# Delta rule: block turns on VectorE and hops through a DRAM buffer in place of TensorE transposes and repeats

## The chip, the cores and the metric

The kernel runs on one core of a Trainium2 chip. The metric is the device time of one execution in microseconds; a kernel's time is the median of its runs. Beside the runs there is one profiled execution, and its rows are what the profile shows. TensorE multiplies matrices, VectorE and ScalarE work elementwise, GpSimd does small copies and issues some DMAs, and SyncE (SP) issues most DMAs. Each engine takes its instructions in order.

## The reference

One inference step of one decoder layer, for 256 prompt tokens and 32 sample tokens (8 sequences of 4), in float32:

```python
proj = x @ w_in                       # 2048 -> 11280 columns: gB gC h q k v z b a m_a m_b
y_a = (gB * conv3(gC * h)) @ w_a_out
q, k, v = split(silu(conv4(concat(q, k, v))))
q, k = l2norm(q), l2norm(k)           # per head, 8 heads of 128
beta = sigmoid(b);  g = -exp(a_log) * softplus(a + dt_bias)
o, S = gated_delta_rule(q, k, v, g, beta, S0)
o = o * rsqrt(mean(o * o) + eps) * gdn_norm_w * silu(z)
y_b = o @ w_b_out
x = layer_norm(ALPHA * x + (sig(m_a) * y_a + sig(m_b) * y_b) @ w_o)
x = layer_norm(ALPHA * x + relu(x @ w_up)**2 @ w_down)
```

The delta rule works on chunks of 64 tokens. Per head and chunk it builds a 64x64 triangular matrix from the keys, inverts it, and then walks the chunks with a state S of 128x128:

```python
v_new = u - w @ S
o     = qdec @ S + attn @ v_new
S     = S * exp(glast) + kdec.T @ v_new
```

The prompt has four chunks and starts from S = 0; each sample sequence is one short chunk and starts from its own S0. The outputs are the prompt's and samples' rows, the convolutions' last inputs and the new states.

## The kernel before

**Weight blocks.** All projections are one list of 496 blocks. A block is 512 KB of weights, loaded by SP (line 171) into one of four buffers. ScalarE rounds it to a high half (`hi`, line 179), VectorE subtracts that to get a low half (`lo`, line 186), and TensorE multiplies each 128x128 piece three times (lines 206 to 208): high by high, high by low, low by high. The activations lie turned, with features in the 128 partitions and 288 tokens along the free axis. In the main loop (line 1371), the iteration of block i makes the high half of block i+3, runs one step of the delta rule, makes the low half of block i+3, runs the evacuations that fall due, multiplies block i and issues the load of block i+7. The order on every engine is thus written out by hand.

**Order of the blocks.** First k, q, v of heads 0 to 3 (blocks 0 to 23), then of heads 4 to 7 (24 to 47), then the inputs of mixer A (48 to 95), z (96 to 111), and the merge. Four blocks make a group of 256 columns. Its evacuation (`conv_evac`, line 253) runs in the three blocks after it: GpSimd writes the padding (lines 265, 266), ScalarE copies from PSUM, VectorE does three multiply-adds per 128 columns (line 272), ScalarE applies SiLU. The z group's evacuation (`z_evac`, line 354) multiplies the delta rule's outputs in the tile `ao` in place, two heads at a time, for heads 0 and 1 at block 100, then at 104, 108 and 112.

**The delta rule.** `gdn(G)` (line 919) is a generator that runs twice, for heads 0 to 3 and 4 to 7; each `yield` ends a step, and the main loop takes one step per block. The first half begins in block 20. The second begins when the first is done and its samples' program too. Its parts, with lines of the kernel before:

- Lines 924 to 926: the samples' states S0 (2 MB per half) are loaded by four DMAs that GpSimd issues, at step 0.
- Lines 954 to 965: keys and queries lie as features x tokens. TensorE turns them by 16 transposes per half (line 958); ScalarE squares them and copies the keys to `kdec` (lines 960, 962); VectorE sums the squares (line 963).
- Lines 973 to 987: the samples' keys and queries are turned (two transposes); the samples' keys, repeated four times by GpSimd (`wide`, line 976), are turned by four more (line 980).
- Lines 995 to 1042: decays, norms, the products of keys with keys and queries.
- Lines 1045 to 1121: the triangular inverse. Its first step needs `mx`, of which GpSimd makes the low part (line 1089) after `spread_kq` (line 1063); TensorE takes it at line 1094. `states_of` (line 1068) multiplies S0 by the samples' keys and queries.
- Lines 1136 to 1207: `sample()`, a second generator that runs one step per block beside the first. It solves the samples' small system, repeats the values four times by four matmuls (line 1176), makes `vm` on GpSimd (line 1192) and adds eight products to S0 (line 1203), two per step, each in a PSUM tile of its own.
- Lines 1215 to 1221: values are turned by eight transposes per half.
- Lines 1226 to 1267: the walk over the chunks. `p3` (two tiles) and `p4` (one) hold products in PSUM and are released by VectorE (lines 1262 and 1264).
- Lines 1272 to 1299: the outputs are normalised and turned back by eight transposes per half into `ao`; the samples' part by one.

There are four PSUM tiles of this kind (`gtile`, line 124), taken in turn. A small pool of tags is shared: a new tile of a tag waits until the old one's readers are done.

Of the kernel before, what the change touches and what calls it, by code (L numbers as in the profile page):

```python
# [16 lines left out]
P = 128  # L17
# [86 lines left out]
def hybrid_kernel(ctx: ExitStack, tc: tile.TileContext, A):  # L104
# [11 lines left out]
    gp = pool("gp", 4, space=PSUM)  # L116

# [798 lines left out]
    def four(ap):  # L916
        return ap.rearrange("p (h t) -> p h t", h=4).unsqueeze(2).to_broadcast([P, 4, 4, 32])

    def gdn(G):
# [4 lines left out]
        S0 = pl.tile([P, 4, 8, P], F32, tag="S0", name=nm("S0"))  # L924
        for hh in range(4):
            gps.dma_start(S0[:, hh], A["state_gdn"][0, :, 4 * G + hh].rearrange("b d e -> d b e"))

# [11 lines left out]
        rep4 = sqr[:, 512:1024]  # L939
        junk = sqr[:, 192:320]  # L940
        wide = rep4.rearrange("p (h q t) -> p h q t", h=4, q=4)
# [7 lines left out]
        red = T([P, 4, 4], "red")  # L949
# [4 lines left out]
        for c in range(4):  # L954
            kt = gtile()
            kv = kt.rearrange("p (h c) -> p h c", h=4)
            for hh in range(4):
                pe.transpose(kv[:, hh, :], kq[:, hh, c].rearrange("p s x -> p (s x)"), ident)  # L958
            s2 = sqr[:, 512 * (c % 2):512 * (c % 2) + 512].rearrange("p (h c) -> p h c", h=4)
            act.activation(s2, kv, AF.Square)  # L960
            for par in range(2):
                act.copy(kdec[rows[par], c], kv[rows[par], par::2, :])
            dve.tensor_reduce(out=red[:, c, :], in_=s2, axis=mybir.AxisListType.X, op=ADD)
# [4 lines left out]
        ssv = ss[:, 0:16].rearrange("p (a c r) -> p a c r", a=2, c=4)  # L968
        for par in range(2):
            act.copy(ssv[rows[par], 0], red[rows[par], :, par::2])  # L970
            act.copy(ssv[rows[par], 1], red[rows[par], :, 1 - par::2])
        sp2 = gtile()
        pe.transpose(sp2[:, 0:128], kst, ident)
        pe.transpose(sp2[:, 128:256], qst, ident)

        gps.tensor_copy(wide, four(kst))
        yield
        ktr = gtile()
        for hh in range(4):
            pe.transpose(ktr[:, hh * P:hh * P + P], rep4[:, hh * P:hh * P + P], ident)  # L980
        kr = T([P, 4, P], "kr")
        for u in range(2):
            act.activation(junk, sp2[:, u * P:u * P + P], AF.Square, accum_out=ss[:, 16 + u:17 + u])
# [471 lines left out]
```

## Time and profile before

| what | value |
|---|---|
| runs, median (lowest to highest) | 1708.3 us (1707.88 to 1708.3), 3 runs |
| profiled execution, from first to last instruction | 1703.4 us |
| mean granted TensorE clock | 0.998 |
| instructions | 31106 |
| bytes moved by DMA | 279.18 MB, mean 164 GB/s |
| delta rule, first transposes of the first half | at 92.8 us |
| delta rule, last transpose of the second half | at 436.3 us |

The profiled execution's own time outside the span is not recorded; the median of the runs stands 4.9 us above the span. A row of a group of instructions gives line, engine, operation, the tiles written and read, their shape and count, then the busy time, the mean of one in ns, and the idle time before them with what ended it. A row of the timeline gives start and length in us, and in brackets the idle time before it. A row of the chain in order of time gives start and length of one piece of the chain that ended last. A row of a window gives, for a stretch of time, the busy us of TensorE, its weight loads, VectorE, ScalarE and GpSimd with their instruction counts, then granted clock, DMA share and GB/s. A row of a DMA gives tiles, issuing queue, count, size and the median us from issue to landing.

### The profile page before, as it was taken

The page shows a single profiled execution, that of the slowest core. Times are in us where ns is not written, and L with a number is a line of the kernel's source. Part 1 is how long each engine was busy: PE and PEld are TensorE (multiplying, and loading weights), DVE is VectorE, ACT ScalarE, POOL GpSimd, SP SyncE. Part 2 cuts the span into 40 slices and gives each one's busy share as a digit, 9 for nine tenths or more (in the row PEclk, how much of TensorE's full clock was granted, in tenths as well). Part 3 has the DMA queues.
Part 4 walks back from the last instruction along what each step waited for, and adds up shares of the span by engine and source line. Part 5 has one row for each costly group of instructions (what it writes and reads, how often), then busy time and mean ns, then how long its engine had stood idle before and what let it go on. Part 6 is the DMA issues. An engine that isn't in the chain of part 4 may idle for free.

```text
span 1703.4 us, 31106 instructions
## 1 busy us (share of the span) xinstructions
PE 1688.5 (99%) x13063; PEld 1668.7 (98%) x13063; DVE 1007.2 (59%) x1296; ACT 734.1 (43%) x1067; POOL 133.8 (8%) x223
## 2 busy tenths in 40 slices
PE   9999999999999999999999999999999999999997
PEld 7999999999999999999999999999999999999997
DVE  5577876758544444456778844566445654466565
ACT  4675626333543333334445533444334433344442
POOL 2232412023300000000010000000000000000000
PEclk9999999999999999999999999999999999999999
DMA  8464456435555555555565555555555555555552
GB/s 244 140 194 139 123 175 200 150 115 180 162 170 169 166 162 170 163 164 165 158 190 174 165 170 161 164 170 162 167 168 161 163 171 162 164 167 164 162 162 80
DMA packets 275097, 279.18 MB, mean 164 GB/s; under 512 B 13131, under 2 KB 270092, under 8 KB 274952
## 3 DMA queue, kind: packets, MB, share of 16 engines
q1 hardware_dynamic: 270414, 265.95, 51.3%
q0 software_dynamic: 4256, 11.12, 2.3%
q8 instruction: 102, 1.67, 0.4%
q14 instruction: 37, 0.30, 0.1%
q10 hardware_dynamic: 288, 0.13, 0.0%
HBM read 269.68 MB, written 7.48 MB: 163 GB/s over the span
## 4 chain that ended last, share of the span: by engine, by line
PE 98%; DVE 1%; DMA 0%; POOL 0%; issue 0%; SPq 0%; ACT 0%; POOLq 0%; ACTq 0%
PE acc L206 31%; PE acc L208 31%; PE acc L207 31%; PE g L1084 1%; DMA xr<-in_x_prompt_dram 0%; PE g L1072 0%; PE g L1231 0%; PE g L1251 0%; PE g L831 0%; DVE w L143 0%; PE g L1254 0%; PE g L1203 0%; PE g L1243 0%; PE g L608 0%; PE g L798 0%; PE g L958 0%
## 5 line engine op out<-in xcount | busy, mean ns | idle before, releaser
L140 DVE TENSOR_TENSOR lo<-raw,hi 128x1024 fp32r<-128x1024 f32 (+2 forms) x502 | 614.0, 1226 | 556.2 <-ACT hi L179 553.7
L179 ACT CAST hi<-raw 128x1024 fp32r<-128x1024 f32 (+1 forms) x498 | 517.6, 1041 | 765.0 <-PE acc L207 707.7
L206 PE MATMUL acc<-xh,hi 128*128 128x288 f32 x1408 | 422.9, 300 | 0.0
L208 PE MATMUL acc<-xh,lo 128*128 128x288 f32 x1408 | 416.7, 296 | 0.0
L207 PE MATMUL acc<-xl,hi 128*128 128x288 f32 x1408 | 416.5, 296 | 0.0
L206 PE MATMUL acc<-dh,hi 128*128 128x290 f32 x1024 | 303.9, 297 | 0.0
L207 PE MATMUL acc<-dl,hi 128*128 128x290 f32 x1024 | 303.3, 296 | 0.0
L208 PE MATMUL acc<-dh,lo 128*128 128x290 f32 x1024 | 302.7, 296 | 0.0
L206 PE MATMUL acc<-hh,hi 128*128 128x288 f32 x1024 | 302.3, 295 | 0.0
L208 PE MATMUL acc<-hh,lo 128*128 128x288 f32 x1024 | 302.3, 295 | 0.0
L207 PE MATMUL acc<-hl,hi 128*128 128x288 f32 x1024 | 302.3, 295 | 0.0
L206 PEld LDWEIGHTS acc<-xh,hi 128*128 128x128 f32 x1408 | 265.4, 189 | 2.6 <-issue 0.7
L207 PEld LDWEIGHTS acc<-xl,hi 128*128 128x128 f32 x1408 | 265.8, 189 | 0.5
L208 PEld LDWEIGHTS acc<-xh,lo 128*128 128x128 f32 x1408 | 265.6, 189 | 0.0
L206 PEld LDWEIGHTS acc<-dh,hi 128*128 128x128 f32 x1024 | 193.6, 189 | 0.1
L208 PEld LDWEIGHTS acc<-dh,lo 128*128 128x128 f32 x1024 | 193.3, 189 | 0.0
L207 PEld LDWEIGHTS acc<-dl,hi 128*128 128x128 f32 x1024 | 193.3, 189 | 0.1
L207 PEld LDWEIGHTS acc<-hl,hi 128*128 128x128 f32 x1024 | 192.5, 188 | 0.0
L208 PEld LDWEIGHTS acc<-hh,lo 128*128 128x128 f32 x1024 | 192.3, 188 | 0.0
L206 PEld LDWEIGHTS acc<-hh,hi 128*128 128x128 f32 x1024 | 192.1, 188 | 0.0
L207 PE MATMUL acc<-ml,hi 128*128 128x288 f32 x256 | 75.6, 295 | 0.0
L208 PE MATMUL acc<-mh,lo 128*128 128x288 f32 x256 | 75.6, 295 | 0.0
(404 smaller groups left out, 1620.0 us busy)
## 6 DMA issues: line engine op xcount, KB each, us to landing
raw<-in_w_in_dram SPq DMA_DIRECT2D x176, 512.0 KB, 3.5
raw<-in_w_up_dram SPq DMA_DIRECT2D x128, 512.0 KB, 3.9
raw<-in_w_down_dram SPq DMA_DIRECT2D x128, 512.0 KB, 3.7
raw<-in_w_o_dram SPq DMA_DIRECT2D x32, 512.0 KB, 3.7
raw<-in_w_a_out_dram SPq DMA_DIRECT2D x16, 512.0 KB, 3.7
raw<-in_w_b_out_dram SPq DMA_DIRECT2D x16, 512.0 KB, 3.6
S<-in_state_gdn_dram POOLq DMA_DIRECT2D x8, 512.0 KB, 7.8
out_dram<-S POOLq DMA_DIRECT2D x8, 512.0 KB, 4.9
```

The costliest lines, as they stand in the source:

```text
L140: dve.tensor_tensor(out=out, in0=a, in1=b, op=op)
L179: act.copy(his[i][:, k:k + step], raw[i][:, k:k + step])
L206: pe.matmul(o, wh, xh_, start=st, stop=False)
L207: pe.matmul(o, wh, xl_, start=False, stop=False)
L208: pe.matmul(o, wl, xh_, start=False, stop=en)
L1084: pe.matmul(out[r, q * 64:q * 64 + 64], a[r, q, :], b[r, q, :], start=True, stop=True)
```

## The change

A DRAM buffer `dp` is added. VectorE's transpose turns each 32x32 block of a tile in its place, so a full 128x128 turn also needs the blocks to change places; DMAs do that on the way to DRAM and back.

- Keys and queries: VectorE turns blocks into `tk` (steps 0 and 1), four SP DMAs write them to `dk` (step 2), four SP DMAs read them back as `kT` and `qT` (step 3). ScalarE squares each in one instruction of 1024 columns, VectorE sums it (step 5). `kdec` is made from `kT` by the multiply that was there.
- Samples' keys and queries: one block turn, eight GpSimd DMAs to `ds` (step 1), one read into `spk` and four reads into `kr` (step 3), which repeat the keys.
- Values: two block turns (step 10), four SP writes (step 11), one SP read (step 12) into `v`, which now lies as four pieces of 32 columns.
- Samples' values: ScalarE copies them out of PSUM, one GpSimd write to `dx`, four GpSimd reads that repeat them.
- Outputs: two block turns into `to`, four SP writes to `do`, eight SP reads into `ao` in pieces of 32 tokens (128 bytes).
- `tk`, `qT`, `kT` and `tv` share the memory of S0 (tag `S0`). S0 is therefore loaded later, at step 13 of the half, when they have been read.
- Step counts: a half has 48 steps after the first instead of 47 (first) and 41 instead of 40 (second); `sample()` begins at step 24 instead of 22 and has three steps more.

The diff, cut to its core:

```diff
+    dp = pool("dp", space=bass.MemoryType.DRAM)
...
-        S0 = pl.tile([P, 4, 8, P], F32, tag="S0", name=nm("S0"))
-        for hh in range(4):
-            gps.dma_start(S0[:, hh], A["state_gdn"][0, :, 4 * G + hh].rearrange("b d e -> d b e"))
...
-        for c in range(4):
-            kt = gtile()
-            kv = kt.rearrange("p (h c) -> p h c", h=4)
-            for hh in range(4):
-                pe.transpose(kv[:, hh, :], kq[:, hh, c].rearrange("p s x -> p (s x)"), ident)
-            s2 = sqr[:, 512 * (c % 2):512 * (c % 2) + 512].rearrange("p (h c) -> p h c", h=4)
-            act.activation(s2, kv, AF.Square)
-            for par in range(2):
-                act.copy(kdec[rows[par], c], kv[rows[par], par::2, :])
-            dve.tensor_reduce(out=red[:, c, :], in_=s2, axis=mybir.AxisListType.X, op=ADD)
-            if c % 2:
+        for hh in range(4):
+            dve.transpose(out=tk[:, :, hh % 2, :, hh // 2],
+                          in_=kq[:, hh].rearrange("p c s x -> p c (s x)").rearrange("p c (j b) -> p j c b", j=4))
+            if hh == 1:
+                dve.transpose(out=ts.rearrange("p u h x -> p (u h x)"), in_=kqs.rearrange("p u h b t -> p (u h b t)"))
+            if hh == 1:
                 yield
+        ds = dp.tile([P, 2, P], F32, tag="ds", name=nm("ds"))
+        for u in range(2):
+            for i in range(4):
+                gps.dma_start(ds[:, u, rows32(i)].rearrange("(h b) x -> b h x", h=4), ts[rows32(i), u])
+        yield
+        dk = dp.tile([P, 4, 2, 256], F32, tag="dk", name=nm("dk"))
+        for i in range(4):
+            sp.dma_start(dk[:, i].rearrange("(j b) a t -> b j (a t)", j=4),
+                         tk[rows32(i)].rearrange("p j a c r x -> p j (a c r x)"))
+        gps.dma_start(spk, ds)
+        for q in range(4):
+            gps.dma_start(kr[rows32(q)], ds[:, 0].rearrange("(h b) d -> b h d", h=4))
...
+        for a in range(2):
+            r = rows[a]
+            sp.dma_start(kT[r].rearrange("p i c r x -> p i (c r x)"), dk[r, :, a])
+            sp.dma_start(qT[r].rearrange("p i c r x -> p i (c r x)"), dk[r, :, 1 - a])
...
-        yield
+        for u, t in enumerate((kT, qT)):
+            s2 = sqr.rearrange("p (q i x) -> p i q x", q=8, i=4)
+            act.activation(s2, t.rearrange("p i c r x -> p i (c r) x"), AF.Square)
+            dve.tensor_reduce(out=ss[:, 8 * u:8 * u + 8], in_=sqr.rearrange("p (q d) -> p q d", q=8),
+                              axis=mybir.AxisListType.X, op=ADD)
+        yield
...
+        for r in range(2):
+            dve.transpose(out=tv[:, :, :, r],
+                          in_=vf[:, r].rearrange("p c a x -> p c (a x)").rearrange("p c (j b) -> p j c b", j=4))
+        yield
+        v = T([P, 4, 4, 2, 32], "v")
+        dv = dp.tile([P, 4, 256], F32, tag="dv", name=nm("dv"))
+        for i in range(4):
+            sp.dma_start(dv[:, i].rearrange("(j b) t -> b j t", j=4),
+                         tv[rows32(i)].rearrange("p j c r x -> p j (c r x)"))
+        yield
+        sp.dma_start(v.rearrange("p i c r x -> p i (c r x)"), dv.rearrange("p i t -> p (i t)").rearrange("p (i t) -> p i t", i=4))
...
+        S0 = T([P, 4, 8, P], "S0")
+        for hh in range(4):
+            gps.dma_start(S0[:, hh], A["state_gdn"][0, :, 4 * G + hh].rearrange("b d e -> d b e"))
         spread_kq(0)
...
-            vtr = gtile()
-            for hh in range(4):
-                pe.matmul(vtr[:, hh * P:hh * P + P], rep4[:, hh * P:hh * P + P], vs, start=True, stop=True)
+            dx = dp.tile([P, P], F32, tag="dx", name=nm("dx"))
+            gps.dma_start(dx, Xs)
...
+            for q in range(4):
+                gps.dma_start(v4[rows32(q)], dx.rearrange("(h b) d -> b h d", h=4))
...
-        for u in range(2):
-            pt = gtile()
-            for w in range(4):
-                pe.transpose(pt[:, w * P:(w + 1) * P], of[:, 4 * u + w, :], ident)
...
+        to = T([P, 4, 2, 4, 32], "kdec")
+        for r in range(2):
+            dve.transpose(out=to[:, :, r], in_=o[:, :, r].rearrange("p c (j b) -> p j c b", j=4))
+        yield
+        do = dp.tile([2, 2, P, 2, 4, 32], F32, tag="do", name=nm("do"))
+        for i in range(4):
+            sp.dma_start(do[1 - i // 2, i % 2].rearrange("(j b) r c x -> b j (r c x)", j=4),
+                         to[rows32(i)].rearrange("p j r c x -> p j (r c x)"))
+        yield
+        for a in range(2):
+            for r in range(2):
+                t0 = gd["ao"][:, 1, 4 * G + a + 2 * r, 0:NP_].rearrange("p (c n x) -> p n c x", c=4, n=2)
+                for n in range(2):
+                    sp.dma_start(t0[:, n], do[a, n, :, r])
```

More of the change, by code (lines that the diff above doesn't have):

```diff
@@ L913, in gates, with rows32 @@
         yield
-    def four(ap):
-        return ap.rearrange("p (h t) -> p h t", h=4).unsqueeze(2).to_broadcast([P, 4, 4, 32])
+    def rows32(n):
+        return slice(32 * n, 32 * n + 32)
     def gdn(G):
@@ L948, in gdn @@
         ss = T([P, 22], "ss")
-        red = T([P, 4, 4], "red")
         kdec = T([P, 4, 2, P], "kdec")
@@ L952, in gdn @@
         rows = (slice(0, 64), slice(64, 128))
[L954 to L965 removed]
+        flat = T([P, 4096], "S0")
@@ L966, in gdn @@
+        for q in range(4):
+            gps.dma_start(kr[rows32(q)], ds[:, 0].rearrange("(h b) d -> b h d", h=4))
         tt(gl, bc(G_["g"][:, :, pr], 64),
            cst("lc").unsqueeze(1).unsqueeze(1).to_broadcast([P, 4, 2, 64]), MUL)
[L968 to L972, printed above, removed]
@@ L993, in gdn @@
         yield
-        yield
+        for u, t in enumerate((kT, qT)):
[3 more added lines that the diff above has]
+                              axis=mybir.AxisListType.X, op=ADD)
+        yield
+        for u in range(2):
+            act.activation(junk, spk[:, u], AF.Square, accum_out=ss[:, 16 + u:17 + u])
+        act.activation(sqr[:, 0:512], kr.rearrange("p h d -> p (h d)"), AF.Square)
+        dve.tensor_reduce(out=ss[:, 18:22], in_=sqr[:, 0:512].rearrange("p (h d) -> p h d", h=4),
+                          axis=mybir.AxisListType.X, op=ADD)
         gr = gtile()
@@ L1168, in sample @@
             yield
-            act.copy(wide, four(Us))
             yield
@@ L1172, in sample @@
             pe.matmul(pv_[:, 0:P], Us, vs, start=True, stop=True)
+            act.copy(Xs, pv_[:, 0:P])
             act.mul(vns, pv_[:, 0:P], sc[:, 1:2])
-            vtr = gtile()
-            for hh in range(4):
-                pe.matmul(vtr[:, hh * P:hh * P + P], rep4[:, hh * P:hh * P + P], vs, start=True, stop=True)
-            vr = sqr[:, 0:512].rearrange("p (h d) -> p h d", h=4)
-            tt(vr, vtr.rearrange("p (h d) -> p h d", h=4), bc(rsc[:, 1], P), MUL)
-            v3 = pl.tile([P, 4, P], F32R, tag="U", name=nm("v3"))
-            lows(v3, vr, 1)
             yield
+            dx = dp.tile([P, P], F32, tag="dx", name=nm("dx"))
+            gps.dma_start(dx, Xs)
             po = gtile()
@@ L1185, in sample @@
             done.append(1)
+            yield
+            for q in range(4):
+                gps.dma_start(v4[rows32(q)], dx.rearrange("(h b) d -> b h d", h=4))
+            yield
+            yield
+            vr = sqr[:, 0:512].rearrange("p (h d) -> p h d", h=4)
+            tt(vr, v4, bc(rsc[:, 1], P), MUL)
+            v3 = pl.tile([P, 4, P], F32R, tag="U", name=nm("v3"))
+            lows(v3, vr, 1)
             vm = {}
```

57 lines of the change are left out of this document (22 added, 35 removed).

## The prediction

> **What bounds the kernel now.** I read the page first: the engines' busy shares, then the chain that ended last.
>
> ```profile
> span 1703.4 us, 31106 instructions
> PE 1688.5 (99%) x13063; PEld 1668.7 (98%) x13063; DVE 1007.2 (59%) x1296; ACT 734.1 (43%) x1067; POOL 133.8 (8%) x223
> PE 98%; DVE 1%; DMA 0%; POOL 0%; issue 0%; SPq 0%; ACT 0%; POOLq 0%; ACTq 0%
> ```
>
> TensorE is busy 99% of the span and is 98% of the chain. So a microsecond taken from TensorE is a microsecond of the result, unless something then comes late. Next I read the chain in order of time, where pipelined matmuls stand with what each adds, not with their latency.
>
> ```profile
> 92.99 0.87 PE g L958 x8
> ...
> 99.92 0.13 PE acc L206
> ...
> 101.12 0.11 PE g L973
> 101.22 0.11 PE g L974
> ...
> 104.53 0.44 PE g L980 x4
> ...
> 180.11 0.87 PE g L1219 x8
> ...
> 201.15 0.89 PE g L1176 x8
> ...
> 271.72 0.87 PE g L1291 x8
> ...
> 283.13 0.87 PE g L958 x8
> ...
> 366.19 0.87 PE g L1219 x8
> ...
> 387.50 0.89 PE g L1176 x8
> ...
> 432.37 0.87 PE g L1291 x8
> ```
>
> From 99.92 to 101.12 stand nine weight matmuls, so one adds 0.133 us, and a block of 24 adds 3.2 us. One turn of a 128x128 tile (L958, L973, L980, L1219, L1291) adds 0.11 us, and all of them stand on the chain. The program runs the delta rule twice, for heads 0 to 3 (from block 20) and 4 to 7 (before: from block 67), one step per weight block.
>
> The last thing to read is how much lateness TensorE does not feel. The split of a block is due three blocks ahead; where VectorE is fullest I take the end of one split and the first matmul that uses it (block 36):
>
> ```profile
> 146.16 1.18 DVE L140 TENSOR_TENSOR lo<-raw,hi 128x1024 fp32r<-128x1024 f32 x1
> ```
> ```profile
> 150.58 0.40 PE L206 MATMUL acc<-xh,hi 128*128 128x288 f32 x1
> ```
> ```profile
> 110.00:150.00 40.00, 40.00 (x359) 39.43 (x359) 37.16 (x67) 25.42 (x46) 10.36 (x23) 1.00 0.48 143
> 300.00:340.00 40.00, 40.00 (x369) 39.22 (x367) 30.79 (x60) 15.32 (x17) 3.60 (x6) 1.00 0.47 142
> ```
>
> The split ends at 147.34, so 3.24 us of cover are left. The two windows give TensorE, weight loads, VectorE, ScalarE and GpSimd. VectorE has 2.84 us idle of 40 in the first half, 9.21 us in the second, where no q, k and v convolutions run beside it.
>
> **The change part by part.**
>
> *Turns and repeats leave TensorE.* Per half: sixteen turns of q and k (two batches at 0.87), two of the samples (0.22), four of the repeated keys (0.44), eight of v (0.87), eight passes that repeat the samples' values (L1176, 0.89), eight of the output (0.87). That is 1.74 + 0.22 + 0.44 + 0.87 + 0.89 + 0.87 = 5.03 us, and 10.06 us for both. What is put in their place issues nothing on TensorE; the products that read v in pieces of 32 keep their number and width, and I cost them at nothing: the columns per matmul stay 128.
>
> *A stall that the change moves.* TensorE's one long wait in the delta rule is this:
>
> ```profile
> 205.81 2.76 POOL vm L1192
> ...
> 210.34 1.73 DVE w L143
> ...
> 215.96 0.79 DVE E L143 x3
> ```
> ```profile
> 216.79 0.50 PE L1203 MATMUL g<-vm,kr 128*128 128x512 f32 x1 [2.99 <-DVE E L143]
> ```
>
> In block 49 the step of the prompt takes three of four PSUM tiles and the samples' products want two more; their release (E, line 1262) stands on VectorE behind a convolution whose padding waited on GpSimd's vm. After the change the samples' program starts two blocks later (24 steps into the half instead of 22), and its products come at its step 11 instead of 8: blocks 55 to 58. The convolutions of q, k and v end at block 50. Five tiles still meet in block 56, so I keep the 0.79 us of the three releases, less what is hidden, 0.7 in all, and gain 2.3. Bounds: gain 0 and 3.0.
>
> *VectorE.* The nearest rows for the new instructions:
>
> ```profile
> L963 DVE TENSOR_REDUCE red<-vmh 128x4 f32<-128x512 f32 x8 | 5.5, 686 | 8.2 <-ACT vmh L960 8.2
> L140 DVE TENSOR_TENSOR xt<-xt,so 128x1024 f32<-128x1024 f32 x2 | 2.5, 1225 | 0.1
> L1102 DVE STREAM_TRANSPOSE xt<-U 128x512 f32<-128x512 f32 x2 | 1.4, 714 | 0.1
> ```
>
> A block turn of 512 columns takes 0.71. Up to step 10 a half gains four of these (2.86), one of 256 (0.36), two sums of 1024 (twice two of 0.686: 2.74) and two turns of v (1.43), and loses four sums (2.74): +4.7 us. TensorE also arrives 2.4 us sooner, since two batches of 0.87, 0.22 and 0.44 are gone. In the second half 9.21 us of idle time and ScalarE's freed copies hide that, at no cost; without this cover it would be the first half's price. In the first half 4.7 + 2.4 stand against 2.84 idle and 3.24 cover: 1.0 us short.
>
> GpSimd adds its part. The state load moves from step 0 to step 13, into GpSimd's queue ahead of spread_kq and mx (L1089), which TensorE's L1094 awaits:
>
> ```profile
> L926 POOL DMA_DIRECT2D S<-in_state_gdn_dram x8 | 7.1, 900 | 0.0
> ```
> ```profile
> 135.91 1.55 POOL L1089 TENSOR_TENSOR mx<-xt,mx 128x512 fp32r<-128x512 f32 x1 [5.34 <-ACT mx L1088]
> ```
> ```profile
> 139.38 0.63 PE L1094 MATMUL g<-mx,bo 128*128 128x512 f32 x2
> ```
>
> mx ends at 137.46, 1.92 us before its use; four issues of 0.9 push it by 3.6, so 1.7 us late. While TensorE waits for mx, VectorE catches up, so the two latenesses overlap. For both I take 2.0 us. Bounds: 0, if VectorE's order change (3 us of it moves from step 10 to 12) and idle time before block 30 suffice; 5.6 if the idle time is not usable (4.7 + 2.4 - 3.24 = 3.9) and both add up. The 13 new small issues on GpSimd in steps 1 and 3 fall into its idle time (29.6 of 40 us above).
>
> *The DMA hops.* Every turn now needs a write to DRAM and a read behind it, on SP's queue between weight loads.
>
> ```profile
> raw<-in_w_in_dram SPq DMA_DIRECT2D x176, 512.0 KB, 3.5
> ...
> S<-in_state_gdn_dram POOLq DMA_DIRECT2D x8, 512.0 KB, 7.8
> ...
> out_dram<-st POOLq DMA_DIRECT2D x4, 24.0 KB, 3.0
> ```
> ```profile
> q1 hardware_dynamic: 270414, 265.95, 51.3%
> ...
> L179 ACT CAST hi<-raw 128x1024 fp32r<-128x1024 f32 (+1 forms) x498 | 517.6, 1041 | 765.0 <-PE acc L207 707.7
> ```
> ```profile
> 436.12 0.37 SPq L171 DMA_DIRECT2D raw<-in_w_in_dram  x1
> ```
> ```profile
> 430.59 1.22 DVE L140 TENSOR_TENSOR xt<-xt,so 128x1024 f32<-128x1024 f32 x1
> ...
> 445.46 0.81 DVE L143 SCALAR_TENSOR_TENSOR ao<-sz,lnp,ao 128x576 f32<-128x576 f32 x1
> 447.73 1.23 DVE L140 TENSOR_TENSOR lo<-raw,hi 128x1024 fp32r<-128x1024 f32 x1 [1.45 <-ACT hi L179]
> ```
> ```profile
> 456.36 0.29 PE L206 MATMUL acc<-xh,hi 128*128 128x288 f32 x1
> ```
>
> A weight load (block 112, issued at 436.12) is used 20.2 us later and needs about 6 (3.5 to land, 1.04 for hi on ScalarE, 1.23 for lo), so SP may stand still for some 14 us. A hop of q and k is four issues (1.5), a landing (3.0), four issues (1.5), a landing (3.5): 9.5 us, and ScalarE squares the result three blocks (9.6 us) after the write; what waits behind it there are the hi halves of later blocks, which have VectorE's cover. Nothing. v's is used twelve steps later: nothing. The samples' keys and values hop on GpSimd, which waits for two landings (6 us); behind it stand the convolutions' padding copies (ScalarE waits for those) and vm, whose products come two blocks after it: nothing, and 2 us at most in the GpSimd term's bound. The state is needed six steps (20 us) after its issue; four loads that land in 7.8 each and overlap fit: nothing, and 2 MB late by all of 7.8 would be the bound.
>
> The output hop is the tight one in the second half. Its multiply ended at 431.8; two blocks later (6.4) and with two turns (1.4) that is 439.6; write 3.0, eight issues 3.0, landing 3.0: about 451 on the old clock. The z gate of heads 4 and 5 needs it at 445.46, with the VectorE queue behind it: the weight splits. The split behind it ends at 448.96 and is used at 456.36, so 7.4 us of cover against a wait of about 6. I take 0.4. The pieces of 128 bytes are not in the trace: per packet of about 1 KB the page gives 0.513 x 16 x 1703.4 / 270414 = 52 ns. Eight reads make 4096 packets, 256 per engine: 13.2 us if a small packet costs as much, 1.7 if an eighth. I take it near the low end, since bytes set it; at the high end, with the first six reads needed, the wait grows by 8.7 and the stall is about 7.2. Bounds 0 and 7.2.
>
> [...] A turned tile costs VectorE 0.71 / 4 = 0.18 us and TensorE 0.11. [...]
>
> **Sum.** 1703.4 - 10.06 - 2.3 + 2.0 + 0.4 = 1693.4 for the profiled span. The runs' median is 1708.3, 4.9 above the span; with that the forecast is 1698.3.
>
> **The rivals.**
>
> 1. *All idle time goes, nothing new waits*: -10.06 - 3.0, 1695.2. For it: the cover rows; against it: block 36 has 3.24 us only.
> 2. *VectorE and GpSimd late in the first half*, the upper bound of that term: 1698.3 + 3.6 = 1701.9. For it: 37.16 of 40 us busy; against it: the second half is free of it.
> 3. *The output hop holds the z gate*: 1698.3 + 6.8 = 1705.1, within 0.2% of now.
> 4. *The output hop is dear in both halves: slower.* With 52 ns per small packet a hop is landing 3.0, issues 3.0, data 13.2, landing 3.0: 22 us in which the next weight loads stand behind; over the 14 us of cover that stalls 8 in the first half, and 7.2 to 8 in the second: 1698.3 + 15 = 1713. It outweighs the gain once a hop takes about 19 us. Against it: 512 KB of 1 KB pieces land in 3.5. [...]
> 5. *It does not do what it says*: the freed time becomes waits of equal size in both halves (VectorE sets the pace; its added work, 4.7 and two output turns of 1.43 per half, is then paid out of its 2.84 and 9.21 idle), 1708. Against it: 30.79 of 40 in the second half.
>
> **Chances.** Forecast 0.50, rival 1 0.12, rival 2 0.20, rival 3 0.06, rival 4 0.08, rival 5 0.04. About 0.2% (3.4 us) is what a measurement of this kernel tells from no change: faster means below 1704.9. Forecast, 1 and 2 are faster (0.82, of which I give 0.01 to the edge), 3 and 5 are the same, 4 is slower: 0.81, 0.11, 0.08. The range reaches from rival 1 (0.7 below it, for the 0.4 by which runs differ) to rival 3: 1694.5 to 1705.0; it leaves out part of 3, 4 and 5.
>
> **What would show it.** Right: no rows L958, L1219, L1291, L1176 on TensorE and about 10 us less of it busy; the 2.99 us before L1203 gone or under 1; TensorE idle only near blocks 33 to 38 (about 130 to 150 us) and near the second half's end. Wrong: idle time of TensorE behind lo or hi after the output reads (rival 4), or SP's loads landing later than 14 us; a z gate that waits over 7.4 us (rival 3); block turns well over 0.71 us (rival 2). The forecast falls if TensorE's idle time inside the delta rule grows instead of shrinking.

## The result

The changed kernel takes 1737.1 us (median of 4 runs, 1736.4 to 1739.9) beside 1708.3 for the kernel before on the same chip: 1.0177 times as long, 95% interval 1.0163 to 1.0192. It is slower by about 29 us; the forecast was 1698.3, faster, and the range ended at 1705. A run stands about 1.8 us above its span (1736.57 for 1734.8), so of the 4.9 us that the prediction added to the span of before, 3.1 are by how much its profiled execution was faster than the median one; by medians the loss is 28.8 us, by spans 31.4.

The page of the changed kernel, for the rows of the span, the engines and the chain, and TensorE's granted clock in 40 slices:

```profile
span 1734.8 us, 31067 instructions
PE 1693.1 (98%) x12971; PEld 1668.9 (96%) x12971; DVE 1020.6 (59%) x1308; ACT 725.1 (42%) x1029; POOL 145.3 (8%) x257
PEclk9998999989999999999999999999999999999998
PE 82%; DVE 4%; DMA 2%; issue 1%; ACT 1%; POOL 1%; SPq 1%; POOLq 0%; ACTq 0%; DVEq 0%
```

The span is 31.4 us longer. TensorE's idle time rose from 14.9 us (1703.4 - 1688.5) to 41.7 (1734.8 - 1693.1), by 26.8. Its busy time rose by 4.6 although 10 us of turns and repeats are gone, so the rest of its work ran 14.7 us longer: 26.8 + 14.7 - 10.1 = 31.4. Other engines now stand on nearly a fifth of the chain. Which waits these are, the view of waits tells (engine, line, what ended the wait: us in all, times, longest):

```profile
PE acc L209 <- DVE lo L141: 10.4, 8, 2.9
PE g L1116 <- POOL mx L1111: 10.2, 2, 6.0
PE g L1264 <- ACT U L1143: 4.3, 2, 2.2
PE g L1264 <- DVE v L144: 2.2, 4, 1.0
...
PE g L1229 <- DVE E L144: 1.0, 2, 0.9
...
ACT vmh L992 <- DMA S<-dk: 14.7, 2, 8.6
...
DVE ao L144 <- DMA ao<-do: 10.4, 1, 10.4
```

L1229 is the line 1203 of before: the 2.99 us stall there is down to 0.9, as forecast. The other lines shown are new. ScalarE waits 8.6 and 6.1 us for the hop of keys and queries, VectorE 10.4 us for the output hop, TensorE for the low halves behind both, for `mx`, and for U and v at the first chunk.

**The hop of keys and queries**, first half, in the timelines of SP and of ScalarE and VectorE:

```profile
99.96 3.41 SPq L972 DMA_DIRECT2D dk<-S  x4
103.66 0.49 SPq L172 DMA_DIRECT2D raw<-in_w_in_dram  x1
108.42 0.64 SPq L982 DMA_DIRECT2D S<-dk  x1
...
111.12 0.61 SPq L983 DMA_DIRECT2D S<-dk  x1
111.78 10.12 SPq L172 DMA_DIRECT2D raw<-in_w_in_dram  x3
```
```profile
115.67 1.06 ACT L992 ACTIVATE vmh<-S 128x1024 f32<-128x1024 f32 x1 [6.11 <-DMA S<-dk]
```
```profile
116.76 1.22 DVE L993 TENSOR_REDUCE ss<-vmh 128x8 f32<-128x1024 f32 x1 [6.38 <-ACT vmh L992]
```

The writes start at 99.96, and ScalarE gets the data at 115.67: 15.7 us, where the steps leave 9.6. The reads wait for the writes to land (4.1 us is the longest of SP's waits for `dk<-S`) and go out at 108.42, and SP's weight loads stand behind them until 111.78. The DMA rows (count, size, median us to landing) and the windows (last two columns: DMA share, GB/s) say why:

```profile
dk<-S SPq DMA_DIRECT2D x8, 256.0 KB, 6.6
S<-dk SPq DMA_DIRECT2D x8, 256.0 KB, 5.8
...
do<-kdec SPq DMA_DIRECT2D x8, 128.0 KB, 3.9
ao<-do SPq DMA_DIRECT2D x16, 64.0 KB, 2.7
```
```profile
100.00:104.00 4.00, 4.00 (x32) 4.00 (x31) 3.74 (x6) 3.02 (x7) 1.63 (x3) 0.95 0.98 289
104.00:108.00 4.00, 4.00 (x32) 4.00 (x31) 1.84 (x3) 2.49 (x5) 2.05 (x8) 0.95 0.84 243
108.00:112.00 4.00, 4.00 (x31) 3.96 (x30) 2.31 (x4) 1.05 (x1) 0.83 (x1) 0.95 0.91 215
112.00:116.00 4.00, 4.00 (x32) 3.95 (x31) 0.00 (x0) 0.33 (x1) 0.00 (x0) 0.95 1.13 212
```

A half's hop is 1 MB out and 1 MB back, beside a weight stream that fills about half of the DMA engines (share 0.49 from 92 to 96 us); together they are nearly full for 16 us (shares 0.84 to 1.13). (The clock column's 0.95 stands in this profile nearly throughout and costs nothing: from block 120 on, ten blocks take 31.87 us in both profiles.) From 112 to 116 VectorE does nothing at all.

**The slow clock.** At 154 us TensorE has waited 6.03 us for `mx`. Its timeline and two windows (the third column from the end is the granted clock):

```profile
154.05 0.79 PE L1116 MATMUL g<-mx,bo 128*128 128x512 f32 x1 [6.03 <-POOL mx L1111]
154.65 0.44 PE L207 MATMUL acc<-xh,hi 128*128 128x288 f32 x1
154.88 0.44 PE L208 MATMUL acc<-xl,hi 128*128 128x288 f32 x1
...
160.16 0.35 PE L209 MATMUL acc<-xh,lo 128*128 128x288 f32 x1
160.35 0.30 PE L207 MATMUL acc<-xh,hi 128*128 128x288 f32 x1
```
```profile
152.00:156.00 4.00, 1.95 (x7) 1.86 (x8) 1.11 (x3) 1.77 (x4) 2.28 (x9) 0.50 0.99 284
156.00:160.00 4.00, 4.00 (x19) 4.00 (x18) 3.59 (x13) 1.64 (x5) 0.32 (x2) 0.50 1.05 302
```

For 5.5 us the clock is 0.50 and weight matmuls follow each other at 0.24 us instead of 0.133. The wait cost its 6 us and 2.5 us more.

**The wait for `mx`** has its own hop. In GpSimd's timeline:

```profile
148.51 3.54 POOL L1108 DMA_DIRECT2D S<-in_state_gdn_dram  x4 [5.93 <-DMA raw<-in_w_in_dram]
152.04 0.65 POOL L1084 COPY b<-kqs 128x32 f32<-128x32 f32 x4
152.75 1.25 POOL L1111 TENSOR_TENSOR mx<-xt,mx 128x512 fp32r<-128x512 f32 x1
```

The state load stands ahead of `mx`, and it goes into memory that v's turned blocks (`tv`) occupy until v's write has landed. The row names a weight load. But v's read, which has to wait for the same writes, leaves SP 0.8 us before the state load begins (0.7 us before it in the second half, 346.18 and 346.90):

```profile
147.74 0.34 SPq L1063 DMA_DIRECT2D v<-dv  x1
```

The first experiment takes this dependency away.

### The profile page after: what moved, and what is told of

It is laid out like the page before. It is cut to its first block, busy times and chain, and to the rows that moved or that the text cites. A ratio compares the mean times of both kernels' runs of the same rounds, so it can differ in the third digit from the quotient of the medians.

```text
span 1734.8 us, 31067 instructions
## 1 busy us (share of the span) xinstructions
PE 1693.1 (98%) x12971; PEld 1668.9 (96%) x12971; DVE 1020.6 (59%) x1308; ACT 725.1 (42%) x1029; POOL 145.3 (8%) x257
## 4 chain that ended last, share of the span: by engine, by line
PE 82%; DVE 4%; DMA 2%; issue 1%; ACT 1%; POOL 1%; SPq 1%; POOLq 0%; ACTq 0%; DVEq 0%
PE acc L207 26%; PE acc L208 26%; PE acc L209 26%; DVE lo L141 1%; PE g L1103 1%; DVE w L144 1%; DMA dk<-S 0%; PE g L1091 0%; DMA S<-dk 0%; DMA do<-kdec 0%; SPq L1321 0%; DVE v L144 0%; DMA dv<-S 0%; ACT hi L180 0%; DMA raw<-in_w_in_dram 0%
## 5 line engine op out<-in xcount | busy, mean ns | idle before, releaser
L207 PEld LDWEIGHTS acc<-xh,hi 128*128 128x128 f32 x1408 | 269.0, 191 | 2.5 <-issue 0.7
```

The lines of the kernel that those rows point to most:

```text
L207: pe.matmul(o, wh, xh_, start=st, stop=False)
```

## The experiments

Times are medians with the ratio to the kernel before (1706.3 to 1707.4 in these runs) and its 95% interval.

**1. The state load freed of v's hop (s0_early).**

```diff
-        tv = flat[:, 0:1024].rearrange("p (j c r x) -> p j c r x", j=4, c=4, r=2)
...
+        S0 = T([P, 4, 8, P], "S0")
+        for hh in range(4):
+            gps.dma_start(S0[:, hh], A["state_gdn"][0, :, 4 * G + hh].rearrange("b d e -> d b e"))
         yield
         while cur[0] < mark["kqv_end", G] + 3:
             yield
+        v = T([P, 4, 4, 2, 32], "v")
+        tv = v
...
         yield
-        S0 = T([P, 4, 8, P], "S0")
-        for hh in range(4):
-            gps.dma_start(S0[:, hh], A["state_gdn"][0, :, 4 * G + hh].rearrange("b d e -> d b e"))
         spread_kq(0)
```

> The changed kernel, but v's turned blocks are put into v's own tile instead of S0's memory, so the state load no longer waits for v's write to DRAM, and it is issued three weight blocks earlier. Theory 1 (each hop lands after its reader's step; the reader's wait holds its engine's queue; a long wait of TensorE is followed by some 6 us at half clock): TensorE's waits for mx, 10.2 us in two, go, and with them the 6 us at half clock behind the first (2.5 to 4 us of it lost): 1737 - 13 = 1724, between 1720 and 1729. Rival A (VectorE's added work sets the pace): mx was only the place where the lateness showed; the 10 us turn up as waits for lo and the time stays within 4 us of 1737. Rival B (the hops' issues and transfers delay the weight loads): the same as rival A, since no hop is taken away.

1727.2 us, 1.0119 (1.0104 to 1.0134): about 10 us less. TensorE's wait for `mx` fell from 10.2 to 4.5 us. Theory 1 holds for this term. The edit also issues the load three blocks earlier, so it doesn't tell the memory from the place in the queue.

**2. Squares later (kq_late), reads later too (rd_late).**

```diff
         tt(glx[:, 1], glf, glx[:, 0], SUB)
         yield
+        yield
+        yield
         for u, t in enumerate((kT, qT)):
...
             yield
-            if G == 0:
-                yield
```

The last edit drops four empty steps of the first half's chunks.

> The changed kernel with the squares of keys and queries two weight blocks later (two empty steps ahead of them in each half, made up in the first half by four empty steps less at its chunks). The hop took 15.7 us where 9.6 were left, so two blocks more (6.4 us) cover it. Theory 1: ScalarE's two waits of 6 to 8.6 us for the hop nearly vanish, the late lo halves of blocks 28 to 33 and 76 to 80 with them (3.7 us of TensorE's time in the first half, 4.7 in the second, and some slow clock): 1737 - 9 = 1728, between 1724 and 1732; the waits for mx (10.2 us) stay. Rival A: the lo halves stay late, 1735 to 1740. Rival B: the same as rival A, with weight loads that land late as the sign.

1738.0 us, 1.0178 (1.0161 to 1.0195): nothing gained in all, the expectation missed. ScalarE's wait for the hop is gone, but its wait for weights is longer (28.6 us in the changed kernel), and a low half is still late, in block 33 instead of 29. From the view of waits:

```profile
ACT hi L180 <- DMA raw<-in_w_in_dram: 49.7, 17, 6.7
...
PE g L1266 <- DVE v L141: 5.4, 1, 5.4
```

The second row says where the gain went. By the starts of their first matmuls, blocks 20 to 39 take 7.7 us less than in the changed kernel (78.6 for 86.3); 2.6 us of this is a shorter wait for `mx`. Blocks 40 to 49 take 8.2 us more (54.6 for 46.3): the first chunk waits 5.4 us for the scaled v, which VectorE makes only behind a convolution that takes 4.88 us there. So the time was lost at a second place, and the total says little of the first.

In rd_late the four reads follow two steps later as well.

> The kernel of the run before with the squares two blocks later, and now the four reads of the hop of keys and queries are issued two blocks later too. In that run the reads stood on SP's queue from the end of the block's weight load (103.82 us in the sibling with all shifts) until the writes had landed (108.79), and the next eight weight loads behind them went out at 111.6. Theory 1b: what costs is the reads' wait on SP's in-order queue, which holds the weight loads; with the reads issued after the writes have landed, the weight loads go out in time, ScalarE's wait for raw (5 to 6 us near 113 to 119 us) goes, and the lo halves of blocks 28 to 33 and 76 to 80 come in time: 1738 - 9 = 1729, between 1724 and 1733. Rival C (bytes: 1 MB written and 1 MB read beside the weight stream load the DMA engines, wherever the reads stand): the lateness moves with the reads, 1735 to 1741. Rival A (VectorE's added work): 1735 to 1741, lo halves late with no wait of ScalarE.

1739.1 us, 1.0191 (1.0175 to 1.0207): missed again, with the same two parts (7.1 us less in blocks 20 to 39, 7.8 more in 40 to 49). SP did not stand still, but issued three weight loads before the reads, which left it at 109.3 us, hardly later than in the changed kernel (108.4). They took longer to land, so that ScalarE waited for them once more (its timeline, and the DMA rows):

```profile
120.55 1.06 ACT L994 ACTIVATE vmh<-S 128x1024 f32<-128x1024 f32 x1 [4.73 <-DMA S<-dk]
```
```profile
dk<-S SPq DMA_DIRECT2D x8, 256.0 KB, 8.1
S<-dk SPq DMA_DIRECT2D x8, 256.0 KB, 8.7
```

So it isn't SP's order alone (theory 1b). That the reads take longer behind more weight bytes fits rival C, that the bytes decide.

**3. The output turned by TensorE again (out_pe).**

```diff
-        to = T([P, 4, 2, 4, 32], "kdec")
-        for r in range(2):
-            dve.transpose(out=to[:, :, r], in_=o[:, :, r].rearrange("p c (j b) -> p j c b", j=4))
...
+        for u in range(2):
+            pt = gtile()
+            for w in range(4):
+                pe.transpose(pt[:, w * P:(w + 1) * P], of[:, 4 * u + w, :], ident)
```

> The changed kernel with the output turned back by TensorE and copied by ScalarE, as before, instead of the hop. TensorE gets 1.74 us of turns back. Theory 1: the z gate's 10.4 us wait of the second half goes, and with it the lengthening of blocks 112 to 116 (2.4 + 1.2 + 3.0 us): 1737 + 1.7 - 6.6 = 1732, between 1730 and 1735; the rest of the loss stays. Rival A: VectorE loses two block turns per half, 2.9 us in all, of which under 3 us come back: 1736 to 1739. Rival B: sixteen DMAs less on SP, weight loads earlier everywhere behind block 60: below 1728.

1727.6 us, 1.0123 (1.0108 to 1.0138): by the ratios (1.0177 - 1.0123) x 1707 = 9.2 us less, though TensorE does 1.74 us more; twice what theory 1 gave, and a missed expectation (1730 to 1735). The time is just under rival B's 1728, but not by its mechanism: in the profiles blocks 60 to 109 are no shorter (210.1 us instead of 208.4), and blocks 110 to 119 are 6.7 us shorter, 32.17 instead of 38.86.

**4. All shifts at once (all3, best1, best2).**

all3 joins the edits of 1 and 2 and drops seven empty steps of the first half. best1 adds the later reads, puts the scaling of v ahead of the inverse's last three stages, and gives the first chunk an empty step instead:

```diff
         aux.append(sample())
-        vq = v.rearrange("p i c r x -> p i (c r) x")
-        tt(vq, vq, bc(bmid(nr[:, 0:8], 4), 32), MUL)
+        yield
```

best2 is best1 with TensorE's output turns.

> The changed kernel with both shifts at once: the state load three blocks earlier with v turned in its own tile, the squares two blocks later, and in the first half seven empty steps dropped, so that the second half starts earlier and its output hop has more time before the z gate. Every new instruction and DMA of the change stays. Theory 1: all three places of lateness go; of 26.8 us more waiting and about 14.6 us of slow clock nearly all come back, the 10 us of turns stay saved: 1698 to 1708. Rival A: VectorE's work is as large as before, so the waits come back at other places: over 1720. Rival B: the DMAs are as many as before: over 1720, with weight loads landing late.

> The kernel with all shifts (1722.4), with three more: the reads of keys and queries two blocks later, an empty step again ahead of the first chunk, where the change had dropped one, and the scaling of v five steps earlier. Every new instruction and DMA of the change is still there. Theory 1b: the late lo halves (7 to 8 us of waits), the wait of the first chunk's products for v and U (5.4 and 2.2 us) go, and the slow clock behind them: 1722 - 16 = 1706, between 1700 and 1711. Rival C or A: the lo halves stay late, only the chunk's wait goes: 1714 to 1720.

> The same as the kernel before it in this list, with the output turned back by TensorE. 1.74 us of turns more, no output hop. Theory 1b: if the output hop at its earlier place costs nothing any more, 1.7 us slower than its sibling; if it still delays weight loads in both halves, faster by 1 to 6 us.

all3 1722.4 us, 1.0088 (1.0073 to 1.0103); best1 1719.9, 1.0074 (1.0056 to 1.0092); best2 1711.9, 1.0031 (1.0022 to 1.0041). The expectations of theory 1 for all3 and best1 were too good; both came out where the rivals had them (over 1720, and 1714 to 1720). all3 has the 5.4 us wait for the scaled v too. In best1 the waits of the first chunk for U and v are gone (a step stands again where the change had dropped one behind v's turns, and v is scaled earlier), but the low halves still come late:

```profile
PE acc L209 <- DVE lo L141: 11.5, 6, 5.0
```

best2, without the output hop, is 8.0 us faster than best1, beyond its expectation of 1 to 6. Most of this is not the z gate: 7.1 us lie in blocks 70 to 79 (36.1 us instead of 43.2), at the start of the second half. There, in best1, the first half's output reads on SP end 2.6 us before the second half's keys are written, and the longest wait of the row above (5.0 us) is in block 74. That the two hops get into each other's way is inferred from this:

```profile
276.11 5.02 SPq L1322 DMA_DIRECT2D ao<-do  x8
...
283.75 2.02 SPq L971 DMA_DIRECT2D dk<-S  x4
```

**5. The price of a wait (mx_wait32),** on the kernel before:

```diff
+        for _ in range(32):
+            gps.memset(kso, 0.0)
         gps.tensor_tensor(out=mx[:, 1], in0=Xf, in1=mx[:, 0], op=SUB)
```

> The kernel before the change, with 32 fills of a tile of 256 columns (about 0.33 us each, 10.6 us in all) on GpSimd ahead of mx in each half; nothing else differs and the fills are not used. mx was ready 1.92 us ahead of its reader, so TensorE waits some 8.7 us in each half. Theory 1: behind a wait of that length TensorE's matmuls run at half the granted clock for some 6 us, which costs 3 us more each time: 1708 + 2 x (8.7 + 3) = 1731, with a granted clock near 0.5 in the windows behind the waits. Rival D (a wait costs its length, the slow clock comes from something else): 1708 + 17.4 = 1725 or less, clock 1.00 behind the waits.

1713.1 us, 1.0037 (1.0023 to 1.0051), 18 us under the expectation. The waits were shorter than expected: 3.86 us in the first half and none in the second. But the clock did what theory 1 says:

```profile
139.76 0.39 PE L1096 MATMUL g<-mx,bo 128*128 128x512 f32 x1
144.01 0.50 PE L1096 MATMUL g<-mx,bo 128*128 128x512 f32 x1 [3.86 <-POOL mx L1091]
...
144.49 0.44 PE L207 MATMUL acc<-xl,hi 128*128 128x288 f32 x1
...
147.61 0.42 PE L208 MATMUL acc<-xh,lo 128*128 128x288 f32 x1
```
```profile
144.00:148.00 4.00, 3.99 (x17) 3.94 (x18) 2.85 (x11) 2.41 (x5) 0.92 (x5) 0.57 0.00 0
148.00:152.00 4.00, 4.00 (x33) 4.00 (x32) 3.69 (x11) 1.49 (x3) 0.25 (x2) 1.00 0.00 0
```

Blocks 30 to 39 grew by 5.6 us for a wait of 3.9. No DMA moved in these two windows, so transfers beside the matmuls are not what slows them; rival D falls.

**6. One suspect at a time, added to the kernel before.** vec_extra adds the block turns on VectorE, unused; hop_unread adds the writes and reads of the keys' and queries' hop, read by nobody; pe_double issues each of TensorE's 16 turns of keys and queries twice.

```diff
+            dve.transpose(out=vx[:, 0:512], in_=kq[:, c].rearrange("p c s x -> p (c s x)"))
...
```
```diff
+                sp.dma_start(dk[:, i].rearrange("(j b) a t -> b j (a t)", j=4),
+                             kq[rr].rearrange("p h c s x -> p h (c s x)"))
...
+                    for _ in range(2):
+                        sp.dma_start(vx[rows[a]], dk[rows[a], :, a])
```
```diff
-                pe.transpose(kv[:, hh, :], kq[:, hh, c].rearrange("p s x -> p (s x)"), ident)
+                for _ in range(2):
+                    pe.transpose(kv[:, hh, :], kq[:, hh, c].rearrange("p s x -> p (s x)"), ident)
```

> The kernel before the change, with the change's block turns added on VectorE at the same steps (per half four of 512 columns, one of 256, two of 512 for v, two of 512 for the output; 0.71 us for 512: 6.1 us per half), their results unused; nothing is taken away from TensorE. Rival A (VectorE's added work sets the pace): the 12 us show in the time wherever VectorE is full, in the first half above all: 1706.5 + 6 to 12 = 1712 to 1718. Theory 1c: the idle time and the cover of 3 to 6 us take nearly all of it: 1706.5 to 1709.5.

> The kernel before the change, with the DMAs of the hop of keys and queries added to each half at the same steps: four writes of 256 KB to DRAM and four reads of 256 KB behind them on SP's queue. TensorE still turns the tiles, and nothing waits for what is read, so neither ScalarE nor VectorE has more to do. Theory 1c (the hop's bytes fill the DMA engines beside the weight stream, so the hop lands late, and it costs because its reader waits in the middle of the queues of ScalarE and VectorE): without a reader it costs little, 0 to 3 us: 1706.5 to 1709.5. Rival B (the weight loads behind the hop on SP come late and cost by themselves): the lo halves of blocks 28 to 34 and 76 to 80 are late as in the changed kernel, +7 to +13 us: 1713 to 1719.

> The kernel before the change, with each of the 16 turns of keys and queries per half issued twice on TensorE. This measures the price of one: at 0.11 us each, as the chain of waits showed, 32 turns more cost 3.5 us: 1706.5 + 3.5 = 1710. If turns were hidden behind the weight loads of TensorE or behind waits, 1706.5 to 1708, and the 10.06 us that the change was to save would have been less from the start.

- vec_extra: 1707.1 us, 1.0005 (0.9996 to 1.0014). VectorE's 10 us more (busy 1017.4 instead of 1007.2) cost nothing; rival A falls, as far as the block turns go.
- hop_unread: 1710.7, 1.0022 (1.0012 to 1.0031): some 4 us, a little above theory 1c's 3 and well under rival B's 7. Its reads go to the same memory twice, and SP's weight loads behind them went out only at 119.8 us (111.8 in the changed kernel); TensorE waited 1.1 us once. So bytes and SP's wait alone are about half of the hop's price (2.0 to 5.3 us by the interval, of 8.2 below); that the rest comes with the readers is inferred.
- pe_double: 1710.7, 1.0025 (1.0015 to 1.0035), 2.6 to 6 us for 3.5 expected. The turns do stand on the path.

In all three profiles half clock follows the stall of 3.0 us in block 49 (0.57 from 216 to 220 us in vec_extra, 0.56 in pe_double, 0.57 from 220 to 224 in hop_unread), in that of before it doesn't (1.00). The windows behind it, before and vec_extra:

```profile
216.00:220.00 4.00, 3.21 (x23) 3.17 (x24) 4.00 (x8) 0.53 (x2) 2.56 (x2) 1.00 0.35 117
```
```profile
216.00:220.00 4.00, 2.52 (x10) 2.42 (x11) 3.96 (x10) 0.54 (x2) 1.57 (x1) 0.57 0.47 131
```

**7. Parts that have time (mix), and one hop added to them.** mix keeps the samples' and v's turns and hops, and leaves keys, queries and outputs to TensorE; the state load is back at the half's start, four empty steps are dropped in the first half and one added ahead of the first chunk. mix_out adds the output hop to mix, mix_qk that of keys and queries. Against the changed kernel, mix has in its core:

```diff
-        flat = T([P, 4096], "S0")
+        S0 = T([P, 4, 8, P], "S0")
+        for hh in range(4):
+            gps.dma_start(S0[:, hh], A["state_gdn"][0, :, 4 * G + hh].rearrange("b d e -> d b e"))
...
-            dve.transpose(out=tk[:, :, hh % 2, :, hh // 2],
-                          in_=kq[:, hh].rearrange("p c s x -> p c (s x)").rearrange("p c (j b) -> p j c b", j=4))
...
+                pe.transpose(kv[:, hh, :], kq[:, hh, c].rearrange("p s x -> p (s x)"), ident)
```

> Of the change only what has time for its hop: the samples' keys and values, and v (turned in its own tile, scaled five steps earlier). Keys, queries and outputs are turned by TensorE as before; the state load stands at the half's start as before; four empty steps less in the first half's chunks, one empty step ahead of the first chunk. TensorE saves per half 0.22 + 0.44 + 0.87 + 0.89 = 2.42 us, 4.84 in all. Theory 1c: with no hop on a path that is due, no wait of TensorE over 1.5 us is left in blocks 28 to 50 and 76 to 100 and at the end; the stall of 3 us of the sample's products can stay (it did at 3.5 us in the other kernel with fewer empty steps): 1706.4 - 4.8 = 1701.6, between 1699 and 1705, faster than both kernels. Rival A or C: the waits come back though two hops of four are gone: 1706 to 1712.

> The kernel mix (1703.4) with the change's output hop in place of TensorE's turns of the output; TensorE saves 1.74 us more. By the prediction's step (0.4 us lost): 1702. Theory 1c (two writes and reads of 1 MB in all fill the DMA engines, and the z gate in VectorE's queue waits for them): the second half of mix starts some four blocks earlier than in the changed kernel, so the z gate's wait is shorter than 10.4 us but not nothing: 1703 to 1709.

> The kernel mix with the change's hop of keys and queries in place of TensorE's turns, at the change's steps (reads one block after the writes, squares two blocks after the reads; the state load behind its last reader). TensorE saves 1.74 us more. By the prediction's step (nothing lost): 1701.6. Theory 1c: the reader waits 6 to 9 us in each half, the lo halves behind it are late by 3 to 4 us, with slow clock behind: mix - 1.7 + 10 = 1712, between 1708 and 1716.

- mix: 1703.4 us, 0.9978 (0.9970 to 0.9987), as expected and faster than both kernels. One wait of over 1.5 us is left, against the expectation: 2.8 us for ScalarE in block 47.
- mix_out: 1702.7, 0.9976 (0.9967 to 0.9986); once more 1701.9, 0.9970 (0.9959 to 0.9982), in the run below. Theory 1c (1703 to 1709) was too high; the prediction's step, 0.4 us lost, gave 1702.
- mix_qk: 1709.8, 1.0015 (1.0005 to 1.0025): 6.4 us more than mix, with 1.74 us less on TensorE. The hop of keys and queries costs 8.2 us, predicted at nothing.

The output hop that cost 11 us in the changed kernel (9.2 + 1.74) costs some 0.3 to 1.4 here (mix_out is 0.7 us faster than mix, 0.3 by the ratios, and 1.4 in its second run, for 1.74 us less of TensorE's work); these differences are within the intervals. In the changed kernel the multiply ahead of it ends at 462.2 and the z gate is due at 470.5 (where it runs in out_pe); it runs at 480.90. In mix_out, whose second half begins earlier by the steps dropped in the first, the multiply ends at 429.5 in block 104 and the wait is short. Nor does a hop of keys follow the first half's output there, as it does in best1; which of the two counts for how much, no run separates. VectorE's timeline in the changed kernel and in mix_out:

```profile
480.90 0.82 DVE L144 SCALAR_TENSOR_TENSOR ao<-sz,lnp,ao 128x576 f32<-128x576 f32 x1 [10.41 <-DMA ao<-do]
```
```profile
446.94 0.82 DVE L144 SCALAR_TENSOR_TENSOR ao<-sz,lnp,ao 128x576 f32<-128x576 f32 x1 [2.76 <-DMA ao<-do]
```

mix and mix_out also differ in the clock. The same wait of 2.81 us in block 47 is followed by full clock in mix and by half clock in mix_out, and blocks 40 to 49 take 46.2 and 48.9 us:

```profile
204.00:208.00 4.00, 3.74 (x29) 3.74 (x30) 2.69 (x6) 3.15 (x8) 0.81 (x3) 1.00 0.46 131
```
```profile
204.00:208.00 4.00, 2.91 (x13) 2.91 (x14) 2.73 (x5) 3.91 (x9) 0.53 (x1) 0.54 0.48 131
```

**8. Still more time for the keys' hop (mix_qk4):** best2 with reads three and squares seven steps behind the writes in the first half, and a step less ahead of TensorE's output turns, for room.

```diff
-        yield
-        yield
+        for _ in range(4 if G == 0 else 2):
+            yield
         for u, t in enumerate((kT, qT)):
```

> The kernel with shifts and TensorE's output turns (1711.9, named best2), in which the squares come two blocks later than in the change, with two blocks more again in the first half (reads three blocks after the writes, squares four blocks after the reads; one empty step less ahead of the output's turns, for room). Theory 1c (lack of time): ScalarE's wait for the hop in the first half, 4.9 us there, is gone, and the lo halves of blocks 31 and 33, late by 2.0 and 3.3 us, come in time: 1711.9 - 5 = 1707, with the second half as it was. If the bytes or VectorE's work cost, wherever the reader stands: 1710 to 1713.

1719.7 us, 1.0074 (1.0059 to 1.0089): both expectations missed. Where the hop is, it did help: blocks 20 to 39 take 4.8 us less than in best2, by the start of their first matmuls. But the rest of the half came later and lost 9.8 us in blocks 50 to 69, with new waits of the chunks for v (5.5 us in four) and of the output's turns (4.3 us in two; the step taken away stood there). It is kq_late's pattern again.

**9. Is it the saved work? (drop4)** mix also drops four empty steps; drop4 drops them alone, on the kernel before.

```diff
-            if G == 0:
-                yield
```

> The kernel before the change with the four empty steps of the first half's chunks dropped, as in mix and mix_out, and nothing else. If their gain is that of the saved TensorE work: 1706.6, within 1.5 us (the work is the same; the stall of 3 us in block 49 can move or change). If it comes from the shorter first half: 1702 to 1704, like mix.

> The kernel mix_out once more, beside drop4 on the same chip: 1702.7, within 1 us. If the saved work is what counts, it lies 3 to 5 us under drop4; if the dropped steps are, both lie together.

drop4: 1709.5 us, 1.0013 (1.0004 to 1.0022), slower than before and than expected (1706.6, within 1.5). mix_out lies 7.6 us under it, more than the 3 to 5 expected, at 6.6 us of saved turns and repeats (2.42 + 0.87 per half). So the dropped steps alone are not the gain, and it has the size of TensorE's saved work. The two kernels also differ in the empty step ahead of the first chunk and in the earlier scaling of v, which were not tried alone.

## Why the prediction was wrong

- **Right: what bounds the kernel.** TensorE's turns stand on the path: pe_double, and mix_out against drop4. **Right:** the stall in block 49 goes (2.99 to 0.9); a block turn of 512 columns takes 0.69 us (0.71 forecast); the samples' hops cost nothing clear of noise (mix gains 2.2 to 5.1 us by its interval, for 4.84 saved); the 128-byte pieces are not dear (`ao<-do` lands in 2.7 us, so rival 4's 13 us of data aren't there). Rival 5's ground, VectorE's added turns, is refuted by vec_extra.
- **Wrong, first: the hop of q and k at 9.5 us, and at no cost ("Nothing").** It took 15.7. The landings were taken from a store of 24 KB (3.0) and a load of 512 KB that ran with the DMA engines half free (3.5); 1 MB each way beside the weights landed in 6.6 and 5.8. And "ScalarE squares the result three blocks (9.6 us) after the write" was no cover: those squares are the head of the half's serial chain (norms, decays, inverse, chunks). A wait there holds ScalarE and VectorE with the weight splits behind; a later step pushes the chain into what follows (kq_late, rd_late, mix_qk4). Price in mix_qk: 8.2 us.
- **Wrong, second: the state load.** "1.7 us late", with VectorE 2.0 for both, bound 5.6. The VectorE part was nothing (vec_extra). The GpSimd part counted four issues of 0.9 but not what they wait for: the load's memory is v's, until v's write has landed. TensorE waited 6.0 and 4.2 us; s0_early gave 10 us back. "v's is used twelve steps later: nothing" looked at v's reader and overlooked the load that waits for its memory.
- **Wrong, third: the output hop at 0.4.** From the end of the multiply to the gate the forecast of 451 has 19.2 us, and 18.7 were measured (462.2 to 480.9); but the terms it lists add to 448.6, 16.8 us, so part of this agreement is luck: the writes' issue (3.5 us) is not among them, and the eight reads took 5.6 us to issue, not 3.0. What failed is the date. It was set against the multiply at 431.8, in block 104 (its matmuls began at 429.0); the change makes each half one step longer, and the multiply came in block 106 (begun at 460.2). The gate was due 8 us after it, not 14, so the wait was 10.4 instead of 6, over the cover of 7.4. Rival 3 named this, at 6.8 us and 0.06. No rival named the other cost, seen in best1: the first half's output hop just ahead of the second half's hop of keys.
- **Not in the sum: the dropped step ahead of the first chunk,** 4.3 us of waits for U. best1 and mix, which give a step back and scale v earlier, don't have them; the two were not tried apart.
- **Not in the sum: the clock.** Every wait was costed at its length. After waits of 3.9 us in mx_wait32 and 6.0 us in the changed kernel TensorE ran at half clock for 3.4 and 5.5 us. Of the 14.7 us by which its remaining work lengthened, 8.6 are in weight matmuls that follow each other at 0.2 to 0.3 us (155 of them in the first 530 us, 76 before, each over by its time above 0.133); the other 6 were not traced.

The prices found, 8.2 (keys and queries) + 10 (state load) + 11 (output) + 4.3 (U), make 33.5 of the 38.9 us by medians (28.8 + 10.1), or of the 41.5 by spans (31.4 + 10.1), to be explained; the stall that went adds 2.1 to either. They were not measured in one setting, and the clock joins them; 5 to 10 us stay unassigned. Why the low halves of blocks 31 to 33 still come late in kq_late and rd_late stays open: VectorE is busy there almost throughout from the squares on (in rd_late no gap is longer than 0.94 us from 124 to 142 us), and what would spread that work was not tried.

## What to carry to other kernels

A turn through memory was cheap here on the engine that turns (0.69 us of VectorE for 512 columns) and dear in delay: cost it by its bytes beside the traffic that runs already (16 us for 1 MB each way, and 19 for 512 KB each way with the steps between), and place it only where its reader can be that late: beside a serial chain, never at its head (8.2 us in mix_qk). For each transfer that moves, list what else waits for its memory and what is queued behind its reader. A shift that helps at one place can lose as much at the next (7.7 us gained and 8.2 lost in kq_late), so read the blocks one by one and not the total alone. A wait of the bounding engine can cost more than its length: 3.86 us cost 5.6 in mx_wait32 and 6.03 cost 8.5 in the changed kernel.

## What was not expected of the hardware

- Half clock followed TensorE's waits of 6.03 and 4.17 us in the changed kernel (granted clock 0.50 from 152 to 160 and from 352 to 356 us), of 3.86 us in mx_wait32 (0.57 from 144 to 148) and of 3.53 us in best2 (0.57 from 252 to 256). After shorter ones it came in some executions and not in others: after the stall of 3.0 us in block 49 not in before's but in vec_extra's (1.00 and 0.57 from 216 to 220), after 2.81 us not in mix's but in mix_out's (1.00 and 0.54 from 204 to 208), and in the changed kernel not after the 2.15 us that ended at 199.7 us (0.95 from 200 to 204) but after the 2.15 us that ended at 398.1 (0.65 from 400 to 404). In these runs the slow stretch did not grow with the wait: 3.4 us behind 3.86 in mx_wait32, while behind the 3.0 us in vec_extra both windows from 216 to 224 are slow (0.57 and 0.58).
- In the changed kernel SP takes 0.85 us to issue one of the hop's writes (3.41 for four) and 0.64 for a read, against 0.37 for a weight load of 512 KB.
- The keys' reads took longer to land with three weight loads issued just ahead of them, 8.7 us in rd_late for 5.8 in the changed kernel, where one was.
